# Input LayerNorm of an encoder layer: tile 0's scale and bias by channel, a new order of loads, zeros of q on Pool

## The chip, the cores and the metric

The kernel runs on one core of one Trainium2 chip. The metric is the device time of one execution in microseconds (us), the median of several runs. A core has TensorE (matrix products, into PSUM), VectorE, ScalarE, Pool (GpSimd) and SyncE (SP), which here only issues transfers (DMA). The profile calls them PE, DVE, ACT, POOL and SP, and TensorE's weight loads PEld.

## The reference

A layer of a bidirectional encoder is applied to two sequences, of 512 and 256 tokens of 1024 channels, in float32. What the change touches is the start:

```python
def _layernorm(x, g, b):
    mu = mean(x); var = mean((x - mu) ** 2)
    return (x - mu) * rsqrt(var + 1e-5) * g + b

x = _layernorm(x, ln_in_g, ln_in_b)          # input LN
proj = x @ w_in                              # 1024 -> 3072
bg, cg, hc, q, k, v = split(proj, 6)         # 512 columns each
y = concat(rms(bg * dwconv3(cg * hc)), rms(neighbourhood_attention(q, k, v)))
x = _layernorm(ALPHA * x + y @ w_o, ln1_g, ln1_b)
u = dwconv3(x @ w_up); x = _layernorm(ALPHA * x + (gelu(u1) * u2) @ w_down, ln2_g, ln2_b)
```

## The kernel before, in words

**Stages.** The 768 tokens are six tiles of 128 rows. The opening (lines 183 to 393) loads them, normalises them (`ln_in`), transposes them (`x_t`), projects v (`v_proj`) and prepares operands of the products that follow. Then come q and k with the attention and the gated convolution (from line 396), the output projection and the first LayerNorm (from line 762), the wide FFN projection (from line 860) and the FFN's second projection (line 1062).

**Float32 in parts.** A float32 operand is used as two parts, hi and lo, of a narrower matmul type. `split` (lines 98 to 100) copies hi on ScalarE and subtracts it for lo on VectorE or Pool: in the profile line 99 is the cast to hi, line 100 the subtraction. A product is three products: hi by hi, hi by lo, lo by hi.

**Input LN.** `ln_stats` (lines 196 to 205) takes a tile's mean and variance with two VectorE statistics (line 199) and a power on Pool (line 204). `ln_sq` (215 to 220) takes them with two passes of ScalarE (lines 219 and 210), small VectorE steps (209, 211) and a power on Pool (212). The string `LNS` says which tile uses which: tiles 0 and 1 VectorE, the others ScalarE. `ln_apply` (225 on) then applies them in two VectorE instructions by row: line 230 subtracts the mean and multiplies by the scale gb0, line 233 multiplies by the inverse deviation and adds the bias gb1. gb0 and gb1 are the 1024 scales and biases broadcast to all 128 rows by two transfers (`load_gb`, 191 to 194). The result is stored to DRAM (line 261, `xa_d`, read again for the residual) and transposed by TensorE (line 250, eight blocks of 128x128 into two PSUM tiles "tr"). `x_t` splits the transposed halves into the products' operands. `x_sums` (278 on) forms sums and differences of an even and an odd tile in four tiles "xz" for later products; the string `TI` says whether VectorE or Pool subtracts their lo parts.

**v.** `v_proj` multiplies each half (24 products of 128x128 by 128x512 a tile, line 303) with the eight blocks of v's weights, split by `wv_prep` (the lo parts by the engines in `WE`: Pool for blocks 0, 1, 3 and 6). The result goes through ScalarE and VectorE (308, 309) to DRAM (312).

**Order.** SP's queue is kept in program order. The loads come first: tile 0's rows in two halves, gb0 and gb1, then v's weights w0 to w7 mixed with the other tiles' rows (the string in line 325), then five blocks for the first pair of projection weights (`Pair`, from line 154; two further ones are added onto them by Pool's DMA queue, lines 163 and 164). These wait for buffers of the ring "raw", which v's weights hold. The stores of the tiles and of v follow. The other engines' work is put in order by a scheduler from readiness and program order; the program order is `SEQA` (line 390): "L" is a tile's input LN, "x" its transposes, "v" and "u" the halves of v's product, "w" a block of v's weights, "P" a block of the pair, "T" the sums. Tiles come in the order 0, 2, 1, 3, 4, 5. xr, the tiles' rows, has six buffers.

**Zeros of q.** Line 409 sets qh and ql (128x1536 each) to zero on VectorE before the q columns are split into them (429, 430).

**Channel vectors.** `ch` holds vectors by channel, one column for each 128 channels, among them the scale and bias of the first LayerNorm (g1, b1). That LayerNorm's transposed blocks are scaled by them in lines 842 (VectorE) and 844 (ScalarE).

Of the kernel before, what the change touches and what calls it, by code (L numbers as in the profile page):

```python
# [8 lines left out]
F32 = mybir.dt.float32  # L9
F32R = mybir.dt.float32r  # L10
AF = mybir.ActivationFunctionType
OP = mybir.AluOpType
# [36 lines left out]
def encoder_kernel(ctx, tc, x, lnp, wv, wproj, wo_a, wo_c, wup, wdn, chan, rpb, mask, ident, out):  # L49
# [19 lines left out]
    def f(ap):  # L69
        return ap.bitcast(F32)  # L70
# [9 lines left out]
    def ar(o):  # L80
        return AR[:, o, :, :, 0:384]
# [114 lines left out]
    def ln_stats(src, name):  # L196
        st = const.tile([P, 2, 6], F32, name="st" + name, tag="st", bufs=3)
        for i in range(2):
            V.bn_stats(st[:, i], src[:, i * 512:(i + 1) * 512])
        mv = mvt()  # L200
        V.bn_aggr(mv[:, 0:2], st)
        V.tensor_scalar(mv[:, 0:1], mv[:, 0:1], -1.0, None, op0=OP.mult)
        V.tensor_scalar(mv[:, 2:3], mv[:, 1:2], EPS, None, op0=OP.add)
        G.tensor_tensor(mv[:, 3:4], mv[:, 2:3], expo[:, 0:1], op=OP.pow)
        return mv
# [50 lines left out]
    xo = {}  # L256

    def ln_in(t):
        mv = ln_stats(xr[t], "i") if LNS[t] == "V" else ln_sq(xr[t], ar(6)[:, :, :, 256:384].rearrange("p h k n -> p (h k) n"))
        ln_apply(xr[t], xr[t], mv, gbt[0, 0], gbt[0, 1], V if LNE[t] in "HV" else G, True, G if LNE[t] == "K" else V, LNE[t] == "H")  # L260
        SP.dma_start(xa_d[t * P:(t + 1) * P], xr[t])
        xr[t] = xr[t].rearrange("p (k n) -> p k n", n=P)

    def x_part(t, c):
# [4 lines left out]
            return xo[t]  # L269
        return ar(2 if u else c)[:, :, :, a * P:a * P + P]  # L270

    def x_t(t):
        xr[t] = [transposed(ps.tile([P, 512], F32, name="tr", tag="tr", bufs=4), xr[t][:, 4 * c:4 * c + 4]) for c in range(2)]
        for c in range(2):
            z = x_part(t, c)
            split(z[:, 0], z[:, 1], xr[t][c])
# [12 lines left out]
    def x_t_sums(a):  # L289
        x_sums(*xr[XE[a]], *xr[XO[a]], [a1.tile([P, 4, P], F32, name="xz", bufs=4) for _ in range(4)], a, engs(TI[4 * a:4 * a + 4]))  # L290

    LNS = "VVAAAA"
    TI, LNE = "GGGVGGGGGVVG", "VVVHVH"

    vq = {}
# [19 lines left out]
    load_x(0)  # L315
    idt = const.tile([P, P], F32, name="idt")
    A.dma_start(idt, ident)
    load_gb(0, a1)
    expo = const.tile([P, 12], F32, name="expo")
    V.memset(expo, -0.5)  # L320
    ones = const.tile([P, 2], F32, name="ones")
    V.memset(ones, 1.0)
    wvr = [ring.tile([P, 512], F32, name="raw", bufs=NRAW) for k in range(KT)]
    ch = const.tile([P, chan.shape[1]], F32, name="ch")
    for z in "w0 w1 w2 w3 w4 w5 x1 w6 x2 w7 x3 c0 x4 x5".split():
        n = int(z[1])
        if z[0] == "x":
            load_x((0, 2, 1, 3, 4, 5)[n])
        else:
            SP.dma_start(*((wvr[n], wv[:, n]) if z[0] == "w" else (ch, chan)))  # L330
# [3 lines left out]
    fw = ch[:, 24:24 + 132].rearrange("p (m k) -> p m k", k=3)  # L334
    fb = ch[:, 156:200]
    g1, b1 = ch[:, 200:208], ch[:, 208:216]
    stm = Stream(2)
    SEQB = ("qk0", "ch0", "bb0", "qk1", "ch1", "qk2", "ch2", "qk3", "ch3", "bb2")
    pb = []
# [46 lines left out]
    ORDER = (1, 7, 6, 2, 4, 5, 3)  # L386
    PW = engs("VGVGVVG")
    TA = (0, 2, 1, 3, 4, 5)
    EA = {"L": lambda i: ln_in(TA[i]), "x": lambda i: x_t(TA[i]), "v": lambda i: v_proj(TA[i], 0), "u": lambda i: v_proj(TA[i], 1), "T": x_t_sums, "P": lambda o: pb[0].prep(o, PW[ORDER.index(o)]), "w": lambda k: wv_prep(k, k + 1), "l": lambda n: load_pair()}
    SEQA = "w0 L0 w1 w2 x0 w3 w4 w5 L1 w6 P2 w7 v0 x1 u0 L2 v1 T0 x2 u1 L3 v2 x3 u2 P1 L4 v3 T1 x4 u3 L5 P6 l2 v4 x5 u4 v5 P5 T2 u5 P4 P3 P7"  # L390
    for z in SEQA.split():
        EA[z[0]](int(z[1]))
    a1_close()
# [12 lines left out]
    pt = a2.tile([P, 2, 4, 256], F32R, name="pt")  # L406
    G.dma_start(mk, mask)
    for z in (qh, ql):
        V.memset(f(z), 0.0)
    y_d = dram.tile([2, 4, P, T], F32, name="y_d")  # L410

    cwn = const.tile([P, 4, 3], F32, name="cwn")
# [766 lines left out]
def _layout(i):  # L1179
# [20 lines left out]
    def chan(v):  # L1200
        return v.reshape(-1, P).T

    def chan3(v):
# [1 line left out]

    z["chan"] = np.concatenate([chan3(a["conv_w"][0]), chan(a["conv_b"][0]), chan(a["gn_g"][0]),
                                chan3(a["ffn_conv_w"][0]), chan(a["ffn_conv_b"][0]),
                                chan(a["ln1_g"][0]), chan(a["ln1_b"][0])], 1)
    z["rpb"] = np.pad(a["rpb"][0][:, ::-1, ::-1].reshape(-1), (PADF, 32))
    ms = []  # L1210
    for j in (0, 1, 3):
# [30 lines left out]
```

## Time and profile before

| | us |
|---|---|
| median of three runs | 865.4 |
| the three runs | 865.4, 857.47, 865.75 |
| the profiled execution's own time | 857.87 |
| its span | 856.1 |

The rows further down come from the profiled execution, with times in us from the start of its span. A page lists busy times by engine; windows give busy time by stretch; a timeline has instructions in order, merged where equal ones follow each other, with the idle time of the engine before them and what ended it in brackets. PEclk is TensorE's granted clock, 1.00 being 2.4 GHz.

### The profile page before, as it was taken

How to read it: one execution, taken by the hardware profiler on the slowest of the kernel's cores; microseconds unless marked ns; L12 is line 12 of the kernel's file. 1: busy time of each engine (PE TensorE's matmuls, PEld its weight loads, DVE VectorE, ACT ScalarE, POOL GpSimd, SP SyncE). 2: the span in 40 equal slices, each digit the busy share in tenths (PEclk: the TensorE clock that was granted, in tenths of full speed). 3: DMA queues.
4: the chain of work that ended last, by engine and by line, in shares of the span. 5: the costliest groups of instructions: out<-in, count | busy, mean ns of one | idle time of the engine just before them, and what ended most of it. 6: DMA issues, size and time to landing. Idle time of an engine off the chain costs nothing.

```text
span 856.1 us, 13322 instructions
## 1 busy us (share of the span) xinstructions
PE 814.3 (95%) x4391; PEld 750.1 (88%) x4391; DVE 684.7 (80%) x1335; ACT 494.1 (58%) x1020; POOL 231.3 (27%) x286
## 2 busy tenths in 40 slices
PE   4899999999999999899999999999999999999995
PEld 3678998989898777899999999999999968888884
DVE  6997757877876658788889888888989679995675
ACT  4755655665776448765656565555656357565060
POOL 3565361263402521222333243332211000000102
PEclk9999999999999999899999999999999999999998
DMA  8688868866836740496998998899752199894361
GB/s 323 214 211 212 181 178 201 192 174 145 205 105 217 256 105 20 97 239 180 260 239 229 239 258 229 234 250 231 205 162 87 38 326 367 298 289 167 120 235 74
DMA packets 86421, 171.02 MB, mean 200 GB/s; under 512 B 12848, under 2 KB 26400, under 8 KB 86000
## 3 DMA queue, kind: packets, MB, share of 16 engines
q1 hardware_dynamic: 59552, 110.87, 39.7%
q0 software_dynamic: 25216, 54.74, 28.8%
q10 hardware_dynamic: 1584, 4.56, 1.4%
q8 instruction: 34, 0.56, 0.3%
q14 instruction: 35, 0.29, 0.1%
HBM read 142.70 MB, written 50.48 MB: 226 GB/s over the span
## 4 chain that ended last, share of the span: by engine, by line
PE 72%; DVE 10%; DMA 8%; ACT 4%; issue 3%; POOL 2%; SPq 0%; POOLq 0%; ACTq 0%; DVEq 0%
PE u L180 38%; PE dn L1062 17%; PE r L180 9%; DMA raw<-in_wproj 3%; DVE w L100 2%; DMA acc<-xa_d 2%; PE vp L303 2%; DMA br<-in_rpb 1%; PE O L680 1%; PE S L623 1%; PE tr L250 1%; DMA gb<-in_lnp 1%; DVE AR L100 1%; PE PT L656 1%; ACT sq L210 1%
## 5 line engine op out<-in xcount | busy, mean ns | idle before, releaser
L180 PE MATMUL u<-AR,w 128*128 128x386 f32 (+2 forms) x1908 | 333.7, 337 | 3.3 <-ACT u L957 3.3
L180 PEld LDWEIGHTS u<-AR,w 128*128 128x128 f32 x1908 | 332.4, 190 | 3.7 <-ACT u L957 3.5
L100 DVE TENSOR_TENSOR w<-raw,w 128x512 fp32r<-128x512 f32 x248 | 172.8, 708 | 54.4 <-ACT w L99 53.3
L99 ACT CAST w<-raw 128x512 fp32r<-128x512 f32 x255 | 156.5, 619 | 91.6 <-PE r L180 27.5
L1062 PE MATMUL dn<-w,hs 128*128 128x512 f32 (+1 forms) x714 | 164.2, 391 | 2.0 <-DVE hs L100 1.9
L1062 PEld LDWEIGHTS dn<-w,hs 128*128 128x128 f32 x714 | 132.3, 190 | 33.5 <-DVE hs L100 2.4
L180 PE MATMUL r<-AR,w 128*128 128x384 f32 x840 | 158.6, 341 | 2.5 <-ACT w L99 0.7
L180 PEld LDWEIGHTS r<-AR,w 128*128 128x128 f32 x840 | 145.4, 189 | 4.1 <-ACT w L99 1.0
L364 POOL DMA_DIRECT2D sw_d<-in_wdn x44 | 37.2, 918 | 107.9 <-DMA sw_d<-sw_d 86.2
L887 DVE SCALAR_TENSOR_TENSOR cu<-u,ch,cu 128x385 f32<-128x385 f32 (+1 forms) x88 | 52.1, 613 | 11.4 <-ACT cu L892 7.3
L99 ACT CAST hs<-hr 128x386 fp32r<-128x386 f32 x73 | 37.6, 515 | 36.7 <-DMA hr<-h_d 33.5
L100 DVE TENSOR_TENSOR w<-rw,w 128x512 fp32r<-128x512 f32 x70 | 47.0, 685 | 8.4 <-ACT w L99 8.4
L99 ACT CAST w<-rw 128x512 fp32r<-128x512 f32 x70 | 43.4, 623 | 15.4 <-issue 12.0
L887 DVE SCALAR_TENSOR_TENSOR cu<-cu,fwn 128x385 f32<-128x385 f32 (+1 forms) x88 | 48.5, 613 | 0.4 <-ACT cu L892 0.4
L1084 POOL TENSOR_TENSOR mv<-mv,expo 128x1 f32<-128x1 f32 x6 | 7.3, 1219 | 151.3 <-DVE mv L1085 151.3
L909 POOL DMA_DIRECT2D h_d<-cu x33 | 24.1, 731 | 84.8 <-DVE cu L914 80.0
L100 DVE TENSOR_TENSOR hs<-hr,hs 128x386 fp32r<-128x386 f32 x73 | 40.1, 551 | 5.3 <-ACT hs L99 5.2
L801 PE MATMUL wo<-w,AR 128*128 128x512 f32 x144 | 34.2, 395 | 0.7 <-DVE acc L807 0.7
L822 PE MATMUL woc<-w,AR 128*128 128x512 f32 x144 | 34.7, 397 | 0.0
L801 PEld LDWEIGHTS wo<-w,AR 128*128 128x128 f32 x144 | 26.8, 188 | 7.1 <-DVE acc L807 1.2
L822 PEld LDWEIGHTS woc<-w,AR 128*128 128x128 f32 x144 | 26.8, 188 | 6.1
L303 PE MATMUL vp<-w,AR 128*128 128x512 f32 x108 | 29.3, 417 | 2.7 <-DVE AR L100 1.1
(193 smaller groups left out, 1074.9 us busy)
## 6 DMA issues: line engine op xcount, KB each, us to landing
raw<-in_wup SPq DMA_DIRECT2D x60, 256.0 KB, 6.9
hr<-h_d SPq DMA_DIRECT2D x73, 193.0 KB, 4.7
raw<-in_wproj SPq DMA_DIRECT2D x50, 256.0 KB, 5.1
rw<-in_wup SPq DMA_DIRECT2D x50, 256.0 KB, 6.8
sw_d<-in_wdn POOLq DMA_DIRECT2D x44, 256.0 KB, 9.1
raw<-sw_d SPq DMA_DIRECT2D x44, 256.0 KB, 4.7
raw<-in_wdn SPq DMA_DIRECT2D x33, 256.0 KB, 4.8
h_d<-ho POOLq DMA_DIRECT2D x11, 579.0 KB, 3.8
```

The source lines that it names most:

```text
L99: A.copy(hi, src)
L100: eng.tensor_sub(lo, src, f(hi))
L180: PE.matmul(q, w[:, g, k], AR[:, OPS[i], h, k, n], start=start and m == 0, stop=stop and m == 11, skip_group_check=True)
L210: A.activation(scratch, src, AF.Square, bias=mv[:, 0:1], accum_out=mv[:, 2:3])
L250: PE.transpose(q[:, k], src[:, k], idt)
L303: PE.matmul(q, x_part(t, c)[:, h, k], wvo[4 * c + k][:, g], start=c + m + k == 0, stop=c == 1 and m == 2 and k == 3)
L364: return lambda: G.dma_start(sw_d[j, SW[i]], src, accum_op=OP.add)
L801: PE.matmul(banks[t], yas(h, i, t), wt[k][:, g], start=i == 0 and m == 0, stop=i == 3 and m == 2)
L822: PE.matmul(q, ycs(h, i, t), woc[i][n][:, g], start=i == 0 and m == 0, stop=i == 3 and m == 2)
L887: V.scalar_tensor_tensor(c[:, e, n], u[:, m], w, c[:, e, n], op0=OP.mult, op1=OP.add)
L909: G.dma_start(h_d[j, i:i + n].rearrange("o p n -> p o n"), src)
L1062: PE.matmul(q[:, x], hs[i, j][:, h, cols(a)], wd[i, j][:, g, x], start=i in (1, 7) and j == 0 and m == 0, stop=j == NJ - 1 and m == 2, ski ...
```

## The change

For tile 0 alone, the LN by row only subtracts the mean and multiplies by the inverse deviation (one VectorE tensor_scalar). Its transposed blocks get scale and bias by channel as they leave PSUM, alternating between ScalarE and VectorE, into a new buffer of xr, from which the operands are split. The residual's copy of tile 0 gets scale and bias by row on Pool, then is stored. The loads are put in a new order: channel vectors, v's eight weights, tile 2's rows, gb0 and gb1, then the rows of tiles 1, 3 and 4; those of tile 5 are loaded after the second tile's v. Tile 1's sums are taken by ScalarE. The zeros of q are written by Pool. The channel vectors gain ln_in's scale and bias (16 columns).

```diff
--- before.py
+++ after.py
@@ -256,6 +256,12 @@
     xo = {}
 
     def ln_in(t):
+        if not t:
+
+            mv = ln_stats(xr[t], "i")
+            V.tensor_scalar(xr[t], xr[t], mv[:, 0:1], mv[:, 3:4], op0=OP.add, op1=OP.mult)
+            xr[t] = xr[t].rearrange("p (k n) -> p k n", n=P)
+            return
         mv = ln_stats(xr[t], "i") if LNS[t] == "V" else ln_sq(xr[t], ar(6)[:, :, :, 256:384].rearrange("p h k n -> p (h k) n"))
         ln_apply(xr[t], xr[t], mv, gbt[0, 0], gbt[0, 1], V if LNE[t] in "HV" else G, True, G if LNE[t] == "K" else V, LNE[t] == "H")
         SP.dma_start(xa_d[t * P:(t + 1) * P], xr[t])
@@ -269,7 +275,30 @@
             return xo[t]
         return ar(2 if u else c)[:, :, :, a * P:a * P + P]
 
+    def x_first():
+
+        x = xr[0]
+        z = a1.tile([P, D], F32, name="xr", bufs=6).rearrange("p (c k n) -> p c k n", c=2, n=P)
+        xr[0] = [z[:, c] for c in range(2)]
+        for c, z in enumerate(xr[0]):
+            q = transposed(ps.tile([P, 512], F32, name="tr", tag="tr", bufs=4), x[:, 4 * c:4 * c + 4])
+            for k in range(4):
+                i = 4 * c + k
+                if k % 2:
+                    V.tensor_scalar(z[:, k], q[:, k], g0[:, i:i + 1], b0[:, i:i + 1], op0=OP.mult, op1=OP.add)
+                else:
+                    A.activation(z[:, k], q[:, k], AF.Identity, bias=b0[:, i:i + 1], scale=g0[:, i:i + 1])
+            o = x_part(0, c)
+            split(o[:, 0], o[:, 1], z)
+        x = x.rearrange("p k n -> p (k n)")
+        G.tensor_mul(x, x, gbt[0, 0])
+        G.tensor_add(x, x, gbt[0, 1])
+        SP.dma_start(xa_d[0:P], x)
+
     def x_t(t):
+        if not t:
+            x_first()
+            return
         xr[t] = [transposed(ps.tile([P, 512], F32, name="tr", tag="tr", bufs=4), xr[t][:, 4 * c:4 * c + 4]) for c in range(2)]
         for c in range(2):
             z = x_part(t, c)
@@ -289,7 +318,7 @@
     def x_t_sums(a):
         x_sums(*xr[XE[a]], *xr[XO[a]], [a1.tile([P, 4, P], F32, name="xz", bufs=4) for _ in range(4)], a, engs(TI[4 * a:4 * a + 4]))
 
-    LNS = "VVAAAA"
+    LNS = "VAAAAA"
     TI, LNE = "GGGVGGGGGVVG", "VVVHVH"
 
     vq = {}
@@ -315,16 +344,17 @@
     load_x(0)
     idt = const.tile([P, P], F32, name="idt")
     A.dma_start(idt, ident)
-    load_gb(0, a1)
     expo = const.tile([P, 12], F32, name="expo")
     V.memset(expo, -0.5)
     ones = const.tile([P, 2], F32, name="ones")
     V.memset(ones, 1.0)
     wvr = [ring.tile([P, 512], F32, name="raw", bufs=NRAW) for k in range(KT)]
     ch = const.tile([P, chan.shape[1]], F32, name="ch")
-    for z in "w0 w1 w2 w3 w4 w5 x1 w6 x2 w7 x3 c0 x4 x5".split():
+    for z in "c0 w0 w1 w2 w3 w4 w5 w6 w7 x1 g0 x2 x3 x4".split():
         n = int(z[1])
-        if z[0] == "x":
+        if z[0] == "g":
+            load_gb(0, a1)
+        elif z[0] == "x":
             load_x((0, 2, 1, 3, 4, 5)[n])
         else:
             SP.dma_start(*((wvr[n], wv[:, n]) if z[0] == "w" else (ch, chan)))
@@ -334,6 +364,7 @@
     fw = ch[:, 24:24 + 132].rearrange("p (m k) -> p m k", k=3)
     fb = ch[:, 156:200]
     g1, b1 = ch[:, 200:208], ch[:, 208:216]
+    g0, b0 = ch[:, 216:224], ch[:, 224:232]
     stm = Stream(2)
     SEQB = ("qk0", "ch0", "bb0", "qk1", "ch1", "qk2", "ch2", "qk3", "ch3", "bb2")
     pb = []
@@ -386,8 +417,8 @@
     ORDER = (1, 7, 6, 2, 4, 5, 3)
     PW = engs("VGVGVVG")
     TA = (0, 2, 1, 3, 4, 5)
-    EA = {"L": lambda i: ln_in(TA[i]), "x": lambda i: x_t(TA[i]), "v": lambda i: v_proj(TA[i], 0), "u": lambda i: v_proj(TA[i], 1), "T": x_t_sums, "P": lambda o: pb[0].prep(o, PW[ORDER.index(o)]), "w": lambda k: wv_prep(k, k + 1), "l": lambda n: load_pair()}
-    SEQA = "w0 L0 w1 w2 x0 w3 w4 w5 L1 w6 P2 w7 v0 x1 u0 L2 v1 T0 x2 u1 L3 v2 x3 u2 P1 L4 v3 T1 x4 u3 L5 P6 l2 v4 x5 u4 v5 P5 T2 u5 P4 P3 P7"
+    EA = {"L": lambda i: ln_in(TA[i]), "x": lambda i: x_t(TA[i]), "v": lambda i: v_proj(TA[i], 0), "u": lambda i: v_proj(TA[i], 1), "T": x_t_sums, "P": lambda o: pb[0].prep(o, PW[ORDER.index(o)]), "w": lambda k: wv_prep(k, k + 1), "l": lambda n: load_pair(), "X": load_x}
+    SEQA = "w0 L0 w1 w2 x0 w3 w4 w5 L1 w6 P2 w7 v0 x1 u0 L2 v1 X5 T0 x2 u1 L3 v2 x3 u2 P1 L4 v3 T1 x4 u3 L5 P6 l2 v4 x5 u4 v5 P5 T2 u5 P4 P3 P7"
     for z in SEQA.split():
         EA[z[0]](int(z[1]))
     a1_close()
@@ -406,7 +437,7 @@
     pt = a2.tile([P, 2, 4, 256], F32R, name="pt")
     G.dma_start(mk, mask)
     for z in (qh, ql):
-        V.memset(f(z), 0.0)
+        G.memset(f(z), 0.0)
     y_d = dram.tile([2, 4, P, T], F32, name="y_d")
 
     cwn = const.tile([P, 4, 3], F32, name="cwn")
@@ -1205,7 +1236,8 @@
 
     z["chan"] = np.concatenate([chan3(a["conv_w"][0]), chan(a["conv_b"][0]), chan(a["gn_g"][0]),
                                 chan3(a["ffn_conv_w"][0]), chan(a["ffn_conv_b"][0]),
-                                chan(a["ln1_g"][0]), chan(a["ln1_b"][0])], 1)
+                                chan(a["ln1_g"][0]), chan(a["ln1_b"][0]),
+                                chan(a["ln_in_g"]), chan(a["ln_in_b"])], 1)
     z["rpb"] = np.pad(a["rpb"][0][:, ::-1, ::-1].reshape(-1), (PADF, 32))
     ms = []
     for j in (0, 1, 3):
```

## Rows read from the trace of the kernel before

**Rows 1.** The page, busy us by engine (share of the span) and instructions.

```profile
PE 814.3 (95%) x4391; PEld 750.1 (88%) x4391; DVE 684.7 (80%) x1335; ACT 494.1 (58%) x1020; POOL 231.3 (27%) x286
```

**Rows 2.** Windows of the opening: us, busy (instructions) by engine, PEclk, DMA share, GB/s.

```profile
5.00:10.00 5.00, 0.00 (x0) 0.00 (x0) 2.11 (x5) 0.00 (x0) 0.56 (x1) 1.00 0.82 304
10.00:15.00 5.00, 3.61 (x12) 2.86 (x13) 3.77 (x4) 4.05 (x8) 2.93 (x3) 1.00 1.04 404
...
30.00:35.00 5.00, 3.24 (x15) 2.21 (x14) 5.00 (x8) 3.74 (x7) 3.11 (x4) 1.00 0.79 236
35.00:58.00 23.00, 22.60 (x110) 17.99 (x109) 22.14 (x38) 14.85 (x28) 9.91 (x9) 1.00 0.56 155
```

**Rows 3.** Timeline, tile 0: start, us, engine, line, operation, count [idle before, releaser].

```profile
3.91 1.50 DVE L199 BATCH_NORM_STATS2 sti<-xr 128x6 f32<-128x512 f32 x2 [2.87 <-DMA xr<-in_x]
...
5.97 0.56 POOL L204 TENSOR_TENSOR mv<-mv,expo 128x1 f32<-128x1 f32 x1 [5.53 <-DVE mv L203]
8.67 1.28 DVE L230 SCALAR_TENSOR_TENSOR xr<-xr,mv,gb 128x1024 f32<-128x1024 f32 x1 [2.77 <-DMA gb<-in_lnp]
...
10.51 1.98 ACT L99 CAST w<-raw 128x512 fp32r<-128x512 f32 x3 [8.04 <-DMA raw<-in_wv]
...
11.39 1.97 PE L250 MATMUL tr<-idt,xr 128*128 128x128 f32 x8 [11.39 <-DVE xr L233]
...
13.18 5.12 PE L303 MATMUL vp<-w,AR 128*128 128x512 f32 x15
```

**Rows 4.** Timeline, TensorE: the transposes of tiles 2 and 1, and a product after them.

```profile
21.67 1.04 PE L250 MATMUL tr<-idt,xr 128*128 128x128 f32 x8
...
29.33 1.06 PE L250 MATMUL tr<-idt,xr 128*128 128x128 f32 x8 [0.51 <-DVE xr L233]
...
34.28 2.59 PE L303 MATMUL vp<-w,AR 128*128 128x512 f32 x10 [1.13 <-DVE AR L100]
```

**Rows 5.** Timeline, Pool and VectorE side by side.

```profile
11.20 2.50 POOL L100 TENSOR_TENSOR w<-raw,w 128x512 fp32r<-128x512 f32 x2 [4.67 <-DMA raw<-in_wv]
...
12.52 1.73 DVE L100 TENSOR_TENSOR w<-raw,w 128x512 fp32r<-128x512 f32 x1 [1.19 <-ACT w L99]
...
58.80 2.91 POOL L100 TENSOR_TENSOR AR<-xz,AR 128x512 fp32r<-128x512 f32 x2
58.95 4.55 DVE L100 TENSOR_TENSOR AR<-xz,AR 128x512 fp32r<-128x512 f32 x1
```

**Rows 6.** Groups over the span: count | busy us, mean ns of one | idle before.

```profile
L647 DVE TENSOR_SCALAR pr<-pr,nm 128x256 f32<-128x256 f32 x16 | 5.0, 356 | 0.1
...
L842 DVE TENSOR_SCALAR zt<-tr,ch 128x128 f32<-128x128 f32 x12 | 4.4, 404 | 3.4 <-PE tr L250 3.4
...
L199 DVE BATCH_NORM_STATS2 sti<-xr 128x6 f32<-128x512 f32 x4 | 2.8, 693 | 3.0 <-DMA xr<-in_x 2.9
...
L647 DVE TENSOR_SCALAR pr<-pr,nm 128x128 f32<-128x128 f32 x8 | 2.2, 285 | 0.0
...
L409 DVE MEMSET qh<- 128x1536 f32 x1 | 1.3, 1338 | 0.3 <-issue 0.3
...
L844 ACT ACTIVATE zt<-tr,ch 128x128 f32<-128x128 f32 x36 | 13.9, 460 | 2.3 <-PE tr L250 2.3
...
L460 POOL TENSOR_TENSOR pre<-pre,sq 128x768 f32<-128x768 f32 x6 | 12.1, 2022 | 12.0 <-ACT sq L459 11.9
...
L100 DVE TENSOR_TENSOR w<-raw,w 128x512 fp32r<-128x512 f32 x248 | 172.8, 708 | 54.4 <-ACT w L99 53.3
```

**Rows 7.** Waits (waiter, releaser: us in total, times, longest), and TensorE's timeline and window near 348 us.

```profile
PE r L180 <- DVE st L567: 0.6, 1, 0.6
...
POOL raw L164 <- DMA raw<-in_wproj: 8.0, 1, 8.0
...
348.05 2.50 PE L180 MATMUL u<-AR,w 128*128 128x256 f32 x10 [3.26 <-ACT u L957]
...
347.00:350.00 3.00, 1.96 (x9) 1.96 (x10) 0.92 (x3) 2.49 (x6) 2.46 (x4) 0.54 0.12 16
```

## The prediction

> **What bounds the kernel now.** I read the page's busy shares first: TensorE is busy for 95% of the span [rows 1], so a change in the opening is worth what it moves TensorE's work, and no more. The windows of the opening came next. In 35 to 58 us TensorE is busy 22.60 of 23 us, so whatever brings it there sooner is kept; in 30 to 35 us it has only 3.24 of 5, while VectorE has 5.00 of 5 [rows 2]. The opening therefore has three limits in a row: a wait for data until TensorE first moves, a full VectorE until about 34 us, then TensorE itself. The timeline shows the first: tile 0's sums are at hand at 6.53 (5.97 + 0.56), yet VectorE's first apply starts at 8.67, after 2.77 us of idle that the broadcast rows gb ended. Transposes start at 11.39, v's first product at 13.18 [rows 3]. The second is seen in tile 2 (transposes at 21.67), tile 1 (29.33, just behind VectorE) and the product at 34.28, which waited 1.13 us for VectorE [rows 4].
>
> Durations are those of the profiled execution, 857.87 us (span 856.1 and 1.8 around it). The median of the runs shown is 7.5 us above it; I make the sum on 857.87 and add those 7.5 at the end.
>
> **Step 1, tile 0 no longer waits for gb.** Its two applies (1.28 us each, after the wait) become one tensor_scalar over 128x1024 with two scalars per row. No such row exists. The same operation takes 285 ns for 128 columns and 356 for 256 [rows 6], 0.55 ns a column, so about 0.78 us; the upper bound is the 1.28 of the apply [rows 3]. I take 0.78, the same operation. It starts at 6.6 and ends at 7.4: transposes at 7.4, not 11.39, a gain of 4.0 (3.5 at the upper bound). New on the path is the scale and bias on each transposed half: two blocks on VectorE at 404 ns beside two on ScalarE at 460 [rows 6], so 0.9 us before the first cast; the second half's 0.9 lies under the first half's twelve products. Net: v starts at 10.1, 3.1 sooner. Weights are no obstacle: the first cast waited for w0 until 10.51 [rows 3], behind gb's 1.05 MB, which at 304 GB/s [rows 2] is 3.4 us, so w0 comes near 7.1 (0.4 later for the channel vectors now ahead of it), and the last weights are passed by 2.1 MB less, 5 us at 404 GB/s.
>
> **Step 2, tile 2 now waits for gb.** All other tiles keep the apply by row. In front of gb there now go the weights (2.10 MB), tile 2's rows (0.52) and the channel vectors (0.12), 2.74 MB or 6.8 us at 404 GB/s: gb lands near 15.4 instead of 8.67. Two applies from there end at 18.0, so gb alone would let tile 2's transposes keep the 3.1 us (18.6 instead of 21.67). But Pool is given tile 0's own product and sum over 128x1024. The nearest row is 2022 ns for 768 columns [rows 6], so 2.70 each, 5.4 together. They come ahead of tile 2's power in program order and become ready with gb. If Pool takes them first it is busy from 15.4 to 20.8, the power (0.56 [rows 3]) ends at 21.4, the second apply starts then, and the transposes come at 22.8, 1.1 late. The timeline shows engines taking later work first when it is ready, so either order is possible; I take the middle, 20.7, a gain of 1.0, and keep -3.1 and +1.1 as ends. On SP the store of tile 0 waits for Pool's sum, with tile 2's and v's stores behind it; these have nothing on TensorE's path directly behind them. Tile 5's rows, now loaded after that store because a buffer is reused, are the last wanted; I cost both at nothing.
>
> **Step 3, tile 1's sums.** Two statistics of 693 ns [rows 6] leave a full VectorE, 1.4 us on the way to 29.33 [rows 4]. ScalarE gets two passes instead. It has 0.95 us free in 10 to 15 and 1.26 in 30 to 35 [rows 2], so I cost them at nothing; without that cover the 1.4 are gone.
>
> **Step 4, Pool against VectorE.** With Pool's two subtractions from 11.20 on, a VectorE subtraction took 1.73 us [rows 5], where the mean of its group is 0.71 [rows 6]; beside Pool's run from 58.80 another took 4.55. So the 5.4 us of new Pool work, put where VectorE is full, cost nothing if nothing meets it, up to 3.9 if one instruction is held as at 58.95. I take 1.0, the row in the same stretch. Tile 0's low halves and two of the sums of the first pair now read SBUF instead of PSUM, and are exposed too.
>
> The Trainium skill, SBUF — State Buffer, "Who interferes with whom", says that a VectorE instruction with two SBUF inputs and a GpSimd instruction that reads SBUF exclude each other for whole instructions, and that a GpSimd one that only writes does not hold it. Rows 5 agree with the first half: 12.52 to Pool's end at 13.70 is 1.18 of the 1.73, the rest is the work. By this rule the product and sum by Pool speak against the change, and the zeros by Pool are free for VectorE; no row shows the second.
>
> **Step 5, zeros of q.** Two memsets of 1.34 us [rows 6] leave VectorE near 64 to 67 us. TensorE runs through most of this; its one wait there that VectorE ended is 0.6 us [rows 7]. I take -0.6; ends 0 and -0.6. On Pool a memset costs between VectorE's 1.34 and twice the 2.02 of the 768-column sum, 2.7 to 8.1 for both; the cover is Pool's 8.0 us of waiting for a transfer [rows 7], just before its next DMA issues. Without it they would hold the weights of the next pair.
>
> **Sum.** At 34 us: -1.0 - 1.4 + 1.0 = -1.4; with step 5, -2.0. 857.87 - 2.0 = 855.9, and against the median 863.4.
>
> **Rivals.**
> Everything is kept: Pool takes the power before its product, the two engines do not meet, ScalarE hides tile 1's sums. -3.1 - 1.4 - 0.6 = -5.1: 860.3. For it: TensorE is full from 35 us on. Against it: VectorE is full from 25 us on and can follow only by what leaves it.
>
> It is swallowed: VectorE is the limit to 34 us anyway. The four new blocks cost it 4 x 0.404 = 1.6, more than the 1.4 that leave, tile 2 is no earlier, and the memsets ran under TensorE's products. 0: 865.4. For it: the full VectorE of rows 2; against it: the four blocks fall near 9 us, where it waits.
>
> Slower, by Pool: product and sum go ahead of tile 2's power, and one apply of tile 2 is held behind them as at 58.95. +1.1 + 3.9 - 1.4 = +3.6: 869.0. It decides once tile 2's transposes come more than 1.4 later than 21.67, at 23.1. TensorE would then sit idle for over 3 us between tile 0's products and tile 2's; after 3.26 us idle at 344.8 its granted clock was 0.54 in 347 to 350 [rows 7], near the level of 1.2 GHz, which could add 1.4 us (0.46 of 3.0). Against it: a single 1.05 us block is the rule in this stretch.
>
> That the change does not do what it says: the queue takes the weights no faster because the transfers in flight share it, w0 still lands near 10, and v starts as before. That gives the swallowed case and is counted there.
>
> **How the numbers follow.** Forecast 0.40, swallowed 0.22, slower 0.22, everything kept 0.16. No case by itself passes 1%, 8.6 us, which is about what a measurement of this kernel can tell from no change: the runs shown run from 857.47 to 865.75. That spread decides the rest: a gain of 2 to 5 with a low median passes 1% downward (0.09), a loss of 3.6 with a high one upward (0.05). The range takes in both ends of the runs: 857.87 less 3.9 (between forecast and everything kept) is 854; the median plus 3.1, near the slower case, is 868.5.
>
> **What would show it.** Right: tile 0's tensor_scalar near 0.8 us ending by 7.6; first transposes near 7.4; v's first product near 10; tile 2's transposes between 18.6 and 22.8; the product that stood at 34.28 one to two us earlier, and the same distance at 58. Wrong: a first cast of a weight still at 10; Pool's product and sum right before tile 2's power, with a TensorE gap of over 4 us; a VectorE subtraction of 3 us or more beside them; TensorE waiting on q's zeros after 65 us; tile 5's rows landing after 40 us.

## The result, and the profile after

The changed kernel takes 866.4 us (median of 20 runs, 862.6 to 874.3), the kernel before 862.0 (20 runs beside it, 857.5 to 867.7). The ratio is 1.0063 with an interval of 1.0041 to 1.0086: 5.4 us slower by the ratio (4.4 by the medians), where 2.0 faster was forecast. The profiled execution took 865.79 us with a span of 864.0. All of the loss is there when TensorE starts the products of q and k, and it stays to the end. The first of these, in the timelines before and after:

```profile
58.37 0.34 PE L537 MATMUL r<-AR 128*128 128x384 f32 x1
```

```profile
64.04 0.33 PE L568 MATMUL r<-AR 128*128 128x384 f32 x1
```

5.7 us there, 4.8 at the first score (79.3 and 84.1), 7.5 at the first output projection (263.6 and 271.1), 7.9 at the end of the span. So the opening is what has to be read. (One experiment, e2_late, has a profile of a disturbed execution; only its ratio is read.) Its windows after (columns as in [rows 2]):

```profile
5.00:10.00 5.00, 1.97 (x8) 1.57 (x8) 2.23 (x10) 2.48 (x4) 2.60 (x3) 1.00 0.96 320
10.00:15.00 5.00, 0.00 (x0) 0.00 (x0) 5.00 (x5) 3.62 (x6) 4.04 (x4) 1.00 1.04 415
15.00:20.00 5.00, 0.00 (x0) 0.00 (x0) 3.25 (x4) 3.08 (x6) 5.00 (x3) 1.00 1.03 401
20.00:25.00 5.00, 2.58 (x10) 2.08 (x11) 4.63 (x8) 2.57 (x6) 2.88 (x3) 1.00 0.98 318
24.00:64.00 40.00, 38.81 (x177) 31.15 (x177) 36.24 (x57) 27.32 (x51) 18.05 (x15) 1.00 0.64 172
```

TensorE does tile 0's transposes early, as forecast, and then nothing from 10 to 20 us. From 24 it is nearly full: 38.81 of 40 us. Its full stretch before ran from 35 to 58 [rows 2]. The timeline shows what it waited for (columns as in [rows 3]):

```profile
6.82 0.81 DVE L262 TENSOR_SCALAR xr<-xr,mv 128x1024 f32<-128x1024 f32 x1 [0.67 <-POOL mv L204]
7.25 5.43 ACT L99 CAST w<-raw 128x512 fp32r<-128x512 f32 x8 [4.79 <-DMA raw<-in_wv]
...
7.69 1.97 PE L250 MATMUL tr<-idt,xr 128*128 128x128 f32 x8 [7.69 <-DVE xr L262]
...
9.34 5.60 DVE L100 TENSOR_TENSOR w<-raw,w 128x512 fp32r<-128x512 f32 x4 [1.70 <-ACT w L99]
13.34 1.06 ACT L219 ACTIVATE AR<-xr 128x1024 fp32r<-128x1024 f32 x1 [0.66 <-DMA xr<-in_x]
...
14.75 2.39 POOL L294 TENSOR_TENSOR xr<-xr,gb 128x1024 f32<-128x1024 f32 x1 [0.96 <-DMA gb<-in_lnp]
...
16.18 0.79 ACT L290 ACTIVATE xr<-tr,ch 128x128 f32<-128x128 f32 x2
...
16.43 1.80 DVE L230 SCALAR_TENSOR_TENSOR xr<-xr,mv,gb 128x1024 f32<-128x1024 f32 x1
17.11 1.53 POOL L212 TENSOR_TENSOR mv<-mv,expo 128x1 f32<-128x1 f32 x1
...
18.61 2.33 POOL L295 TENSOR_TENSOR xr<-xr,gb 128x1024 f32<-128x1024 f32 x1
18.67 3.35 DVE L233 SCALAR_TENSOR_TENSOR xr<-xr,mv,gb 128x1024 f32<-128x1024 f32 x1 [0.45 <-POOL mv L212]
...
21.95 0.72 DVE L288 TENSOR_SCALAR xr<-tr,ch 128x128 f32<-128x128 f32 x2
22.08 1.57 PEld L250 LDWEIGHTS tr<-idt,xr 128*128 128x128 f32 x8 [12.82 <-DVE xr L233]
22.08 1.97 PE L250 MATMUL tr<-idt,xr 128*128 128x128 f32 x8 [12.42 <-DVE xr L233]
22.39 0.81 ACT L290 ACTIVATE xr<-tr,ch 128x128 f32<-128x128 f32 x2 [3.99 <-DVE xr L288]
...
22.88 0.76 DVE L288 TENSOR_SCALAR xr<-tr,ch 128x128 f32<-128x128 f32 x2
...
23.72 1.14 ACT L99 CAST AR<-xr 128x512 fp32r<-128x512 f32 x2
...
24.39 2.07 PE L332 MATMUL vp<-w,AR 128*128 128x512 f32 x4 [0.34 <-ACT AR L99]
```

Tile 0's transposes are done at 9.66. Its blocks (lines 290 and 288) are taken up at 16.18 and 21.95. ScalarE has all eight casts of weights and tile 2's two passes (219, 210) ahead of them in its queue. VectorE has four low halves of weights and both of tile 2's applies (230, 233), which wait for gb and for Pool. On TensorE tile 2's transposes stand ahead of tile 0's products. So tile 0, whose data was ready first, went through the engines behind tile 2, and v's first product came at 24.39 against 13.18 [rows 3]. Tile 2's transposes came nearly as before (22.08; 21.67 in [rows 4]).

### The profile page after: what moved, and what is told of

The parts are those of the page before. It is cut to its first block, busy times and chain, and to the rows that moved or that the text cites. A ratio compares the mean times of both kernels' runs of the same rounds, so it can differ in the third digit from the quotient of the medians.

```text
span 864.0 us, 13331 instructions
## 1 busy us (share of the span) xinstructions
PE 813.9 (94%) x4391; PEld 751.0 (87%) x4391; DVE 682.0 (79%) x1333; ACT 498.1 (58%) x1028; POOL 238.7 (28%) x290
## 3 DMA queue, kind: packets, MB, share of 16 engines
q1 hardware_dynamic: 59552, 110.88, 39.6%
## 4 chain that ended last, share of the span: by engine, by line
PE 70%; DMA 10%; DVE 10%; ACT 4%; issue 2%; POOL 2%; SPq 1%; POOLq 0%; ACTq 0%; DVEq 0%
PE u L180 38%; PE dn L1093 15%; PE r L180 10%; DMA raw<-in_wproj 4%; PE vp L332 2%; DMA acc<-xa_d 2%; DVE w L100 2%; PE O L711 1%; DMA raw<-sw_d 1%; PE S L654 1%; DMA vw<-v_d 1%; PE PT L687 1%; DMA gb<-in_lnp 1%; DVE AR L100 1%; DMA br<-in_rpb 1%
## 5 line engine op out<-in xcount | busy, mean ns | idle before, releaser
L100 DVE TENSOR_TENSOR w<-raw,w 128x512 fp32r<-128x512 f32 x248 | 175.0, 718 | 59.8 <-ACT w L99 58.6
L675 ACT ACTIVATE pr<-pr,nm 128x192 f32<-128x192 f32 (+3 forms) x48 | 21.3, 444 | 13.4 <-DVE nm L672 13.4
```

The costliest lines, as they stand in the source:

```text
L100: eng.tensor_sub(lo, src, f(hi))
L675: A.activation(o, o, AF.Exp, bias=nm[:, n:n + 1], scale=-1.0, accum_out=nm[:, 4 + n:5 + n])
```

## The experiments

Four theories stand behind the expectations. A: v's start decides, since TensorE then needs some 39.6 us to q and k (24.39 to 64.04). B: Pool's product and sum, holding VectorE, are the loss. C: VectorE's sum of work sets the stretch to q and k. D: A and C together. One table has what is read from each profile, the start of v's first product and the first product of q and k, and the ratio to before.

| run | v | q and k | ratio [95%] |
|---|---|---|---|
| before | 13.18 | 58.37 | 1 |
| after | 24.39 | 64.04 | 1.0063 [1.0041, 1.0086] |
| e1_first | 17.26 | 62.61 | 1.0068 [1.0041, 1.0096] |
| e2_late | - | - | 1.0109 [1.0078, 1.0141] |
| e3_first_late | 16.18 | 67.66 | 1.0142 [1.0105, 1.0179] |
| e4_vstats | 24.12 | 64.29 | 1.0070 [1.0036, 1.0104] |
| e5_nores | 21.87 | 61.37 | 1.0047 [1.0021, 1.0072] |
| e6_first_nores | 17.26 | 62.41 | 1.0065 [1.0026, 1.0104] |
| e7_gbfirst_first | 21.48 | 65.08 | 1.0110 [1.0051, 1.0169] |
| e8_weave | 11.86 | 65.90 | 1.0124 [1.0077, 1.0171] |
| e9_weave_nores | 11.97 | 62.41 | 1.0069 [1.0026, 1.0112] |
| e10_weave_acc | 12.53 | 66.42 | 1.0128 [1.0080, 1.0176] |
| e11_weave_acc_nores | 12.40 | 62.78 | 1.0095 [1.0060, 1.0129] |
| e12_weave_pw | 12.10 | 61.26 | 1.0046 [1.0014, 1.0079] |
| e13_weave_pw_nores | 11.85 | 58.66 | 0.9992 [0.9962, 1.0022] |
| b1_zero | 12.81 | 58.00 | 1.0009 [0.9978, 1.0040] |
| b2_stats | 12.64 | 56.10 | 0.9985 [0.9949, 1.0020] |
| b3_loads | 20.89 | 61.30 | 1.0026 [0.9988, 1.0064] |
| b4_stats_zero | 13.08 | 58.16 | 1.0012 [0.9980, 1.0044] |

The ratio follows the third column: over the sixteen rows without e2, e10 and e11 (the last two leave work out later on) its correlation with the first product of q and k is 0.97, with v's start 0.30. That says where the loss sits, not what makes it. One caution: b2 and b4 have the same TensorE program up to that product and differ by 2 us there, so a difference under 2 us between two single profiles is not read, and one of 2.6 needs lines of its own beside it.

**The order of issue, and Pool's two instructions.** e1 writes tile 0's blocks ahead of the LN of tiles 2 and 1, by edges that hold an instruction behind another without a wait:

```diff
+        if z == "x0":
+            held["L1"] = held["L2"] = [last(A), last(V)]
+        if z == "v0":
+            held["x1"] = [last(PE)]
```

> The changed kernel with one thing altered: on ScalarE and VectorE tile 0's scale-and-bias blocks and its split are issued ahead of tile 2's statistics and applies, and on TensorE v's first half of tile 0 ahead of tile 2's transposes. Theory A (order: tile 0 is late because it stands behind tile 2's wait for gb in the in-order queues): v's first product at 16 to 18.5 us instead of 24.39, the first q/k product at 58 to 60 instead of 64.04, and the time about 4 to 6 us under the changed kernel's, ratio to before 0.998 to 1.002. Theory B (Pool's product and sum hold VectorE, and that is the loss): first q/k product at 62.5 or later, ratio still 1.004 or more.

e2 puts Pool's product, sum and store ("R0") behind the first pair's sums ("T0"); e3 is both.

```diff
-    SEQA = "w0 L0 w1 w2 x0 w3 w4 w5 L1 w6 P2 w7 v0 x1 u0 L2 v1 X5 T0 x2 u1 L3 v2 x3 u2 P1 L4 v3 T1 x4 u3 L5 P6 l2 v4 x5 u4 v5 P5 T2 u5 P4 P3 P7"
+    SEQA = "w0 L0 w1 w2 x0 w3 w4 w5 L1 w6 P2 w7 v0 x1 u0 L2 v1 T0 R0 X5 x2 u1 L3 v2 x3 u2 P1 L4 v3 T1 x4 u3 L5 P6 l2 v4 x5 u4 v5 P5 T2 u5 P4 P3 P7"
...
+        if z == "T0":
+            held["R0"] = [last(G)]
```

> The changed kernel with Pool's product and sum of tile 0 (and the store, and tile 5's load) put behind the first pair's sums on Pool. Theory A: tile 2's second apply is no longer held (3.35 us becomes 1.28 to 1.6), but tile 0 still stands behind it: v's first product at 21 to 22.5 instead of 24.39, first q/k product at 61 to 62.5 instead of 64.04, ratio 1.002 to 1.005. Theory B: all of the loss goes, first q/k product at 59 or earlier, ratio 0.997 to 1.001.

> Both of the two edits of the other runs. Theory A: v's first product as with tile 0 first alone, 16 to 18.5 us; tile 2's transposes 2 to 4 us earlier than there, first q/k product at 56 to 58.5, ratio 0.996 to 1.000. Theory B: as with Pool's work later alone, within 1 us.

e4 gives tile 1's sums back to VectorE.

```diff
-    LNS = "VAAAAA"
+    LNS = "VVAAAA"
```

> The changed kernel with tile 1's sums on VectorE again, as before the change. If taking the statistics from VectorE helps, as the prediction had it (1.4 us): first q/k product at 65 to 66, ratio 1.007 to 1.009. If ScalarE's two passes for tile 1, which stand among tile 0's blocks, cost more than the statistics: 64 or earlier, ratio 1.006 or less. Theories A and B both expect tile 0 to stay behind tile 2 (v's first product at 23 to 25).

Measured: in e1 v starts 7.1 us earlier and the stretch to q and k gives 5.7 of it back, so its ratio is that of the changed kernel. Part of it is Pool: two subtractions of 0.64 us each were held under Pool's sum.

```profile
17.24 3.59 DVE L100 TENSOR_TENSOR AR<-xr,AR 128x512 fp32r<-128x512 f32 x2 [0.34 <-ACT AR L99]
17.58 2.71 POOL L295 TENSOR_TENSOR xr<-xr,gb 128x1024 f32<-128x1024 f32 x1
```

e2 and e3 are slower than the changed kernel (e2's interval still touches the changed kernel's). In e3 the two Pool instructions ran from 37 us on, where VectorE is full, and held two half applies for 4.43 us; a half apply took 0.75 us at 33.23 in the same run:

```profile
38.91 4.43 DVE L233 SCALAR_TENSOR_TENSOR xr<-xr,mv,gb 128x512 f32<-128x512 f32 x2
```

TensorE waited 2.17 us right behind them, and its granted clock was 0.68 and then 0.64 from 40 to 50 us, so e3's loss is the hold and the clock together. e4 moved nothing that can be read (0.25 us), so in this kernel tile 1's sums on ScalarE show no gain. So A, which fits the changed kernel, falls with e1, and B alone with e2, e3 and e6: moving Pool's two, or leaving them out, does not by itself bring the loss back.

**Without the two Pool instructions.** e5 leaves Pool's two out, so tile 0's part of the residual goes on without scale and bias; e6 is e1 with the same.

```diff
-        G.tensor_mul(x, x, gbt[0, 0])
-        G.tensor_add(x, x, gbt[0, 1])
```

> The changed kernel without Pool's product and sum for tile 0: the residual's copy of tile 0 is stored without its scale and bias. Theory A (start: TensorE runs from v's first product with 39.7 us of work to the first q/k product, as in the changed kernel, so the start decides): v's first product at 21 to 22, because tile 2's second apply is no longer held, and the first q/k product at 61 to 62. Theory C (VectorE: the stretch to the first q/k product is set by VectorE's time, and what Pool's two instructions cost is the time for which they hold it, whenever they run): the same start, and no stop later as in the run that put them behind the first sums (66.83): first q/k product at 60 to 62.5. The time: ratio 1.001 to 1.005 by both.

> Tile 0 ahead of tile 2 in the queues, and no product and sum on Pool (left out of the computation). Theory A: v's first product near 17, first q/k product at 57 to 58.5. Theory C: tile 0 first alone gave 62.61 with VectorE full from 29 us on; without Pool's two instructions VectorE loses 2.3 us less at 17.24 and about 1 us less at 27, so 58.5 to 60: near the 58.37 of the kernel before, not better, although v starts as early as 17. Ratio by A 0.996 to 0.999, by C 0.999 to 1.003.

In e5 tile 2's transposes and all behind them come 2.5 to 2.7 us earlier:

```profile
19.56 1.97 PE L250 MATMUL tr<-idt,xr 128*128 128x128 f32 x8 [9.91 <-DVE xr L233]
21.87 6.97 PE L330 MATMUL vp<-w,AR 128*128 128x512 f32 x24 [0.34 <-ACT AR L99]
```

The rows after say the same: 230 took 1.80 and 233 took 3.35, where each is 1.28 [rows 3], together 2.59 more, both beside Pool's product and sum. Still 3.0 us of the loss at q and k are left, so Pool is not the whole of it, and e6 is no better than e1. That does not make the two instructions free in e1. Without them Pool comes sooner to a transfer that stands ahead of tile 2's power in its queue, one that adds onto a block of weights, and waits there until that block has landed; VectorE's second apply of tile 2 then waits for the power:

```profile
21.27 1.07 POOL L164 DMA_DIRECT2D raw<-in_wproj  x1 [7.13 <-DMA raw<-in_wproj]
```

```profile
23.90 1.28 DVE L233 SCALAR_TENSOR_TENSOR xr<-xr,mv,gb 128x1024 f32<-128x1024 f32 x1 [2.16 <-POOL mv L212]
```

In e6 one wait took the place of another: tile 2's transposes came at 25.24, in e1 at 25.42.

**The loads.** e7 is e1 with gb0 and gb1 loaded first again. b3 is the kernel before with the change's load order and nothing else: gb behind v's weights.

```diff
-    for z in "c0 w0 w1 w2 w3 w4 w5 w6 w7 x1 g0 x2 x3 x4".split():
+    for z in "g0 c0 w0 w1 w2 w3 w4 w5 x1 w6 x2 w7 x3 x4".split():
```

```diff
-    load_gb(0, a1)
...
-    for z in "w0 w1 w2 w3 w4 w5 x1 w6 x2 w7 x3 c0 x4 x5".split():
+    for z in "c0 w0 w1 w2 w3 w4 w5 w6 w7 x1 g0 x2 x3 x4 x5".split():
```

> Tile 0 ahead of tile 2 in the queues, and gb0 and gb1 loaded ahead of v's weights again as before the change (channel vectors behind them). Theory A: weights arrive as before the change, v's first product at 14 to 17, first q/k product at 55 to 57.5. Theory C: tile 2's applies no longer wait for gb, VectorE's idle time at 20 to 25 us goes, but Pool's product and sum still hold it for 2 to 4 us: first q/k product at 58 to 61. Ratio by A 0.994 to 0.998, by C 0.999 to 1.004.

> The kernel before with the change's order of loads alone: the first LN's scale and bias behind v's weights and tile 1's rows, with tile 0 still taking them by row. It prices what the change had to get round. Tile 0's product then waits for them until 14.7 or so, where it ran from 8.7 before: v's first product at 19 to 22. By theory A, with 39.6 us of TensorE from there or 45.2 as before: q and k's first product at 59 to 64, ratio 1.001 to 1.007. By theory C, VectorE idle for some 4 us more ahead of 15 us: 61 to 63, ratio 1.003 to 1.006. If the weights, earlier by the 2 us or so that scale and bias took, make up for it: 58 to 59, ratio 0.999 to 1.001.

In b3 tile 0's first apply starts at 15.20, behind the weights' low halves on VectorE and about when gb lands (issued at 8.52, 6.6 to 7.2 us on its way); its second comes behind tile 2's first. The profile does not separate gb's part from the queue's. v starts at 20.89, and 40.4 us later come q and k:

```profile
15.20 1.29 DVE L230 SCALAR_TENSOR_TENSOR xr<-xr,mv,gb 128x1024 f32<-128x1024 f32 x1
...
17.77 2.48 DVE L233 SCALAR_TENSOR_TENSOR xr<-xr,mv,gb 128x1024 f32<-128x1024 f32 x2
...
19.10 1.97 PE L250 MATMUL tr<-idt,xr 128*128 128x128 f32 x8 [19.10 <-DMA xr<-in_x]
```

Its 61.30 is e5's 61.37: with tile 0 queued behind tile 2, scale and bias by channel gain nothing over taking them by row behind gb, even without Pool's two. The ratio's interval holds 1, so b3 by itself shows the 2.9 us only in the profile. In e7 gb delays the weights (the first cast starts at 10.57), and both the start and the end of the stretch are late.

**The other two edits, on the kernel before.** b1 has q's zeros on Pool, b2 tile 1's sums on ScalarE, b4 both.

```diff
-        V.memset(f(z), 0.0)
+        G.memset(f(z), 0.0)
...
-    LNS = "VVAAAA"
+    LNS = "VAAAAA"
```

> The kernel before with one part of the change alone: the zeros of q on Pool. If it takes 2.7 us from VectorE at no cost (the prediction's step 5): first S product at 78 to 79 instead of 79.3, ratio 0.998 to 1.000. If Pool's memsets hold the weights of the next pair: first S product later than 79.5, ratio above 1.001.

> The kernel before with one edit of the change alone: tile 1's sums and squares by ScalarE in place of VectorE. If VectorE's sum of work sets the stretch to q and k's first product (theories C and D): that product at 57.0 to 58.0 (58.4 before), ratio 0.997 to 1.000. If ScalarE's 0.8 us more stands ahead of its casts of tile 0's blocks: 58.4 to 59.5, ratio 1.000 to 1.002.

> The kernel before with the change's other two edits: tile 1's sums by ScalarE and the zeros of q by Pool; loads, tile 0 and the order of issue as before. If the two add up: q and k's first product at 56 to 57 (58.4 before, 56.1 with the sums alone), first score 0.5 to 1.0 closer to it than the 20.9 us of before, ratio 0.996 to 1.000. If the zeros on Pool bring a wait of their own downstream: first wo later than 264, ratio 1.000 to 1.003.

The interval of each ratio holds 1. b2's 56.10 was not repeated by b4, whose TensorE waited 2.07 us for a weight cast and then had a granted clock of 0.67 from 20 to 25 us. The first score comes 20.9 us behind the first product of q and k before and in b2 (21.0), and 20.1 to 20.2 in after, b1 and b4. But it is 20.0 in b3, where the zeros are still on VectorE (61.30 and 81.28), so these 0.8 us are not shown to be the zeros', and the ratios do not show them.

**The order written out.** e8 puts tile 0's blocks behind the first four weight casts ("x0" behind "w3"), half 0 on ScalarE and half 1 on VectorE, and the rest behind them, Pool's two behind v's first half and ahead of the pair's sums; e9 leaves the two Pool instructions out.

```diff
-                if k % 2:
+                if c:
...
+            held["L1"] = held["L2"] = held["w4"] = held["w5"] = held["w6"] = held["w7"] = [last(A), last(V)]
```

> The changed kernel with the order of issue written out: tile 0's eight blocks right behind the first four casts of v's weights, half 0 all on ScalarE and half 1 all on VectorE; the other four weight casts and the input LN of tiles 1 and 2 behind them; tile 2's transposes behind the first half of v's products of tile 0; Pool's product and sum behind the last weight part and tile 2's root, ahead of the first pair's sums. Two limits (theory D: TensorE needs some 39.6 us from v's first product to q and k's first, and VectorE has a sum of work to do by then, so both an early v and a VectorE that doesn't idle before 30 us are needed): v starts at 12 to 14, q and k's first product at 57 to 59, ratio 0.997 to 1.003. VectorE alone (theory C: it still waits for tile 2's statistics and is held by Pool): v starts as early, but q and k's first product stays at 61 to 63, ratio 1.005 to 1.008. Start alone (theory A): 52 to 54, ratio 0.990 to 0.996.

> As e8_weave, with Pool's product and sum left out (tile 0's part of the residual goes on without the LN's scale and bias by row). It prices these two at a place where VectorE has other work. If their holding of VectorE costs what the profile shows of it there (2 instructions of 2.3 to 2.4 us): q and k's first product 1.5 to 4 us earlier than in e8_weave, ratio lower by 0.002 to 0.004. If they lie in VectorE's waits: within 0.5 us of e8_weave, the same ratio.

v starts at 11.9 as wanted and stops at 18.5 us. In e8, TensorE and Pool:

```profile
24.28 1.22 PE L335 MATMUL vp<-w,AR 128*128 128x512 f32 x2 [5.79 <-POOL w L100]
```

```profile
20.93 1.07 POOL L164 DMA_DIRECT2D raw<-in_wproj  x1 [9.24 <-DMA raw<-in_wproj]
21.69 1.23 POOL L163 DMA_DIRECT2D raw<-in_wproj  x1
22.29 1.93 POOL L100 TENSOR_TENSOR w<-raw,w 128x512 fp32r<-128x512 f32 x1
```

A weight's low half stood behind Pool's accumulating transfer, which waited 9.24 us for its base to land. e10 and e11 put those transfers behind (the two lines of `Pair` that issue them become a step of their own, held behind Pool's last); they also leave out the added transfers of the wide FFN projection's pairs, so only their opening is read.

> As e8_weave, with the first pair's accumulating loads behind Pool's product and sum (in e8 a weight part and tile 2's root stood behind them in Pool's queue, and v's products stopped from 18 to 24 us). Theory D (an early v and a VectorE that doesn't idle before 30 us are both needed, and Pool's product and sum cost what they hold): v's first product at 12, no stop over 2 us before tile 2, tile 2's transposes at 21 to 23, q and k's first product at 57.5 to 60, ratio 0.998 to 1.004. Theory C (VectorE's sum of work sets it whatever the start): 61 to 63, ratio 1.004 to 1.008. Theory A (start alone): 52 to 54, ratio under 0.996.

> As e10_weave_acc, with Pool's product and sum left out (tile 0's part of the residual goes on without the LN's scale and bias by row). The bound of what tile 0's scale and bias by channel can bring here: theory D 55 to 58 for q and k's first product, ratio 0.994 to 1.000, 1.5 to 4 us ahead of e10_weave_acc. Theory C: 60 to 62.5, within 1 us of e10_weave_acc.

The next queue took over. In e11 ScalarE had casts of the first pair ahead of tile 2's, and the pair's rows landed at 23.5:

```profile
23.49 1.14 ACT L99 CAST w<-raw 128x512 fp32r<-128x512 f32 x2 [4.69 <-DMA raw<-in_wproj]
...
26.78 5.49 PE L336 MATMUL vp<-w,xo 128*128 128x512 f32 x12 [5.46 <-ACT xo L99]
```

In the profiles of e8 to e11 the granted clock fell behind these stops: from 25 to 35 us it was 0.56, 0.82, 0.50 and 0.66. Their first products of q and k hold that cost beside the waits, and lie far behind what D expected (65.90, 66.42 and 62.78 in e8, e10 and e11).

e12 and e13 hold these casts behind tile 2's, with nothing left out but the two Pool instructions in e13.

```diff
+        if z == "x1":
+            held["P2"] = held["P1"] = [last(A), last(V)]
```

> As e10_weave_acc with nothing left out, and the first pair's first casts behind tile 2's casts on ScalarE and VectorE (in e10 and e11 tile 2's casts stood behind them on ScalarE and TensorE stopped from about 22 to 27 us). Pool's product and sum still stand ahead of the pair's sums. If waits at the head of a queue are the whole loss: v's first product at 12, tile 2's at 22 to 24, q and k's first product at 58 to 61, ratio 0.999 to 1.005. If VectorE's work, held by Pool, limits: 62 to 66, ratio 1.005 to 1.012.

> As e12_weave_pw with Pool's product and sum left out (tile 0's part of the residual goes on without the LN's scale and bias by row). If waits at the head of a queue are the whole loss: q and k's first product at 56 to 58.5, ratio 0.996 to 1.001; if VectorE's work limits: 60 to 63, ratio 1.003 to 1.007. The distance to e12_weave_pw prices the two Pool instructions: 2 to 4 us at q and k's first product if they hold VectorE for their length, under 1 if not.

In e12 and e13 v's first half runs through. Both ratios lie in the range put down for waits at the heads of queues; the first products of q and k come 0.3 and 0.2 us behind theirs. In e13 and then in e12:

```profile
11.85 8.17 PE L336 MATMUL vp<-w,AR 128*128 128x512 f32 x24 [2.21 <-ACT AR L99]
19.86 1.03 PE L253 MATMUL tr<-idt,xr 128*128 128x128 f32 x8
...
58.66 0.41 PE L595 MATMUL r<-AR 128*128 128x384 f32 x1 [1.53 <-DVE xz L318]
```

```profile
18.49 2.45 POOL L300 TENSOR_TENSOR xr<-xr,gb 128x1024 f32<-128x1024 f32 x1
18.63 3.40 DVE L236 SCALAR_TENSOR_TENSOR xr<-xr,mv,gb 128x1024 f32<-128x1024 f32 x1
21.02 3.23 POOL L301 TENSOR_TENSOR xr<-xr,gb 128x1024 f32<-128x1024 f32 x1
...
22.08 1.09 PE L253 MATMUL tr<-idt,xr 128*128 128x128 f32 x8 [1.88 <-DVE mv L212]
...
61.26 0.41 PE L597 MATMUL r<-AR 128*128 128x384 f32 x1 [1.53 <-DVE xz L320]
```

e13 is level with the kernel before (0.9992 [0.9962, 1.0022]) and clear of the changed kernel's interval. So what it takes out together is the loss: the waits at the heads of queues (with tile 0's blocks now given by halves), and Pool's two instructions. Neither alone is clear of the changed kernel by its ratio (e12 1.0046, e5 1.0047), so how the loss divides rests on the profiles. e12, with Pool's product and sum, is 2.6 us later than e13 at q and k, and its second apply was held for 3.40 us. Between after and e5 it was 2.7, with the granted clock at 1.00 in both. In e12 the clock fell, in e13 it did not (windows of e12):

```profile
20.00:25.00 5.00, 2.41 (x12) 1.77 (x12) 4.29 (x5) 3.46 (x7) 4.92 (x4) 0.89 0.64 243
25.00:30.00 5.00, 5.00 (x22) 4.03 (x21) 4.72 (x7) 2.25 (x5) 3.02 (x4) 0.77 0.95 222
```

Twelve products from 23.89 on took 4.59 us there, 3.02 in e13 (from 22.31), so part of e12's 2.6 may be the clock's. And even with v's start 1.3 us ahead of before, e13 reaches q and k no sooner: TensorE waits there for VectorE (1.53 us), which is busy 28.3 of the 30 us from 30 on:

```profile
30.00:60.00 30.00, 26.72 (x127) 20.99 (x126) 28.30 (x44) 19.41 (x36) 15.34 (x14) 1.00 0.67 196
```

No version is shown to beat the kernel before. b2 has the lowest ratio, 0.9985, and its interval holds 1.

## Why the prediction was wrong

**What bounds the kernel.** That TensorE is full from 35 to 58 us and keeps what is brought to it [rows 2] was right as far as these runs show: 5.7 us late at q and k, 5.4 at the end (0.0063 of 862). The range of 854 to 868.5 holds 866.4 by its width alone, since it reaches from a gain to near the slower rival; the gain and its reason were wrong.

**Step 1 failed at "Net: v starts at 10.1, 3.1 sooner".** All up to it held: sums at hand at 6.8, the tensor_scalar 0.81 us (0.78 taken), transposes at 7.69 (7.4), the first weight cast at 7.25 (7.1). The step then let tile 0's blocks start when their data was ready. They start when their engine's queue comes to them, and the order written into the queues has tile 2's LN ahead. v started at 24.39, and the sum has no term for a later v: these 11.2 us stand nowhere in it. I had read from the timeline that engines take later work first when it is ready; that is the scheduler's order, fixed beforehand from its own estimates of readiness, not a choice on the chip. e1 changes that order alone, and VectorE's first blocks start at 15.22 in place of 21.95. The Trainium skill, PSUM — Partial Sum Buffer, "Engine vs sequencer instructions", calls the queues of ScalarE, VectorE and GpSimd strict FIFO; the trace agrees, since tile 0's blocks on VectorE, transposed by 9.66, began at 21.95, right behind line 233. TensorE idled 12.42 us for that line. Where the order was written out, v started at 11.85 to 12.5. That is still 1.8 or more behind the step's 10.1: ScalarE had weight casts until 9.8 us in e9, and one half's four blocks, all on ScalarE there, took it 1.50 us, where 0.9 was put down for two beside two.

**Step 2** had most parts right and the whole too small: its -1.0 in the sum came out as +0.4 (22.08 against 21.67). gb landed by 14.75 (15.4), Pool's two took 2.39 and 2.33 us (2.70), the power went between them at 17.11, and tile 2's transposes came at 22.08 (20.7, range 18.6 to 22.8). It priced tile 2 alone; with tile 0 queued behind it, tile 2's wait for gb became the wait of every product. b3 has the load order by itself: q and k 2.9 us later in its profile.

**Step 3** took 1.4 us for tile 1's sums. In this kernel they show nothing (e4). I read that as TensorE's late start, not VectorE, setting q and k: 39.65 us from v's first product, and 39.50 in e5; no run shows it by itself. In the kernel before, b2's profile has 2.3 us and its ratio no difference that can be told.

**Step 4** is a term of the sum that was too small: 1.0 us taken, 2.7 and 2.6 measured at q and k (after against e5; e12 against e13, where the clock has a part), and 2.59 on tile 2's two applies themselves, inside the bound of 3.9. Between e1 and e6 it is 0.2, with another wait in its place. One 1.05 us block was taken as the rule of the stretch; Pool's new instructions are 2.4 long, and each of tile 2's applies met one.

**Step 5** took 0.6. No run shows it: b1's ratio does not, and the 0.8 us at the first score are there in b3 without it. The memsets on Pool took 1.41 and 1.40 us (2.7 to 8.1 allowed for both). TensorE did not wait for them; a weight cast on ScalarE waited 3.14 us for the first (70.65), where it idled 3.25 before (65.09):

```profile
69.01 1.41 POOL L440 MEMSET qh<- 128x1536 f32 x1
```

**The rivals.** Slower by Pool was to be decided by tile 2's transposes later than 23.1; they came at 22.08. One apply was held, as it said (3.35 us), but the larger part of the loss was none of its steps. That the change does not do what it says fell with the first cast at 7.25. The swallowed case had v's start kept and its worth lost in VectorE. e13 comes close to that, though tile 2's transposes were earlier there (19.86), and in the orders tried it is the best that the change could have brought. The listed sign of error, a TensorE gap of over 4 us, came three times as long.

What stays open: what holds e1 between v's start and q and k is read as VectorE, 29.02 of 30 us busy from 30 on, and no run takes it away. And the stretch from the first score to the output projection took 184.3 us before and 187.0 after, and from 183.0 (e12) to 191.7 (e4) in the other profiles, on both sides with the zeros on Pool. No edit explains it, so several us of a single profile's end may come from there, and the ends are compared by ratios alone.

## What to carry to other kernels

Data that is ready early is worth only as much as the place of its instructions in each engine's queue: before crediting an early start, walk every engine from there to the product and ask what stands ahead and what that waits for. A wait that is moved from one tile to another (here gb) must be priced for all that is queued behind the new waiter, on every engine. And work given to Pool beside a full VectorE is priced at up to the length of Pool's instruction, not by the shorter holds seen before.

## What the runs showed that was not expected

Blocks of one PSUM tile that were given to ScalarE and VectorE in turn ran one after the other: two on ScalarE at 16.18, two on VectorE at 21.95, then ScalarE again after 3.99 us of idle that VectorE's block ended. A half given to one engine (e8 on) has no such chain. Whether the PSUM tile that both read or the buffer that both write makes it, no run tells.

TensorE's granted clock fell after some gaps and not after others. In the changed kernel it was idle for 12.42 us after 1.97 us of transposes, and the rows from 20 to 25 us have 1.00 (2.4 GHz). In e12 gaps of 1.88 and 0.71 us, after 8.11 us of products, were followed by the 0.77 shown above. In e9, after 6 us of products and a gap of 6.35 us, it was at 0.65 from 25 to 30 (0.50, which is 1.2 GHz, from 24 to 28):

```profile
20.00:25.00 5.00, 0.73 (x2) 0.64 (x3) 0.23 (x1) 1.14 (x2) 4.08 (x5) 0.67 0.86 223
25.00:30.00 5.00, 4.40 (x16) 3.19 (x15) 4.87 (x7) 2.77 (x6) 1.69 (x2) 0.65 0.62 202
```

In b4 a VectorE subtraction that reads two SBUF tiles kept its 0.69 us beside Pool's second memset, but a tensor_scalar of two columns, 154 ns before, took 2.18 and ended with that memset:

```profile
63.13 1.52 POOL L409 MEMSET qh<- 128x1536 f32 x1
63.81 2.18 DVE L416 TENSOR_SCALAR gns<-ch 128x2 f32<-128x2 f32 x1
...
64.45 1.51 POOL L409 MEMSET ql<- 128x1536 f32 x1
...
65.54 0.69 DVE L100 TENSOR_TENSOR w<-raw,w 128x512 fp32r<-128x512 f32 x1
```

The Trainium skill, SBUF — State Buffer, "Who interferes with whom", has both: a two-input VectorE instruction is held by a GpSimd one that reads SBUF and not by one that only writes, while a tensor_scalar can run in a mode that takes the shared ports and so waits for either. Here the trace agrees, and b4's ratio does not show it.
